# Moving the large tiles of a feed-forward pool by 384 bytes: from 416 to 288 modulo 512

## The chip, the core and the metric

The kernel runs on one core of a Trainium2 chip. The metric is the device time of one launch in microseconds (us), the median of several runs; less is better. All inputs are float32. The matrix products run on TensorE (PE) in the type float32r, from operands that VectorE (DVE) and ScalarE (ACT) have split into a high and a low part; SyncE (SP) and GpSimd (POOL) issue most of the DMAs.

## The reference, cut to what matters

One encoder block on 256 tokens of 2048 channels. Only its last half is touched by the change:

```
mix = merged @ w_out                                     # 2048 x 2048
h   = layernorm(ALPHA * x + mix, ln1_g, ln1_b)
ff  = square(relu(h @ w_ff1)) @ w_ff2                    # 2048 -> 8192 -> 2048
out = layernorm(ALPHA * h + ff, ln2_g, ln2_b)
```

Ahead of it stand the input projections (the stages `q`, `k`, `r`, `v`, `g`, `u` below), a gated linear attention, a Hyena convolution, and their output products.

## The kernel before

**How a product is made.** A weight is split into `hi` (a cast to float32r, on ACT) and `lo = weight - hi` (on DVE), the activation likewise; a product is the sum hi·hi + hi·lo + lo·hi. Two loops do this:

- `channel_products` (lines 141 to 153): the weight block is the stationary operand, the activation moves. Line 147 multiplies 128x128 of `whi` with 512 moving columns (256 tokens high and 256 tokens low), line 151 `wlo` with 256 columns. A block of 128 output channels is 16 matmuls of 512 columns and 16 of 256. The stages `q` and `k` and the first feed-forward product (`f<-hT,whi`) go this way.
- `token_products` (lines 188 to 201): the activation is stationary, 512 columns of the weight move. Lines 199, 200, 201 are the three terms. Most other stages go this way, and the last quarter of the second feed-forward product (`w<-whi,fa`).

**The feed-forward stage.** `ff1_first` makes 16 channel blocks of the first product (its first three begin in `begin_three`, lines 173 and 178). Then `ff_pairs` runs 48 slots, each with one channel block of the first product (32 matmuls) and seven "forms" of a seven-product scheme for the second (lines 1243 to 1245, three matmuls of 512 columns for each form: 21 matmuls). So a slot has 37 matmuls of 512 columns and 16 of 256. The stationary operand of the forms lies in `fa`: slots 0 to 3 of eight in `fa0`, 4 to 7 in `fa1` (eight products are summed before the next group starts). Their moving operand is, for three forms, `b_h` and `b_l` (tags `xh` and `wx`), for two `whi` and `wlo`, and for two the tails of `fa0` and `fa1`. After the slots the last quarter runs through `token_products` with `fa` as the stationary operand, half of it in `fa0`, half in `fa1`; its last group takes its weights from resident tiles (`xh_r`, `xl_r`, `fraw_r`, the tails of `fa`, and `wr`, which has the tag `hT`).

**What orders the work.** Inside a slot the instructions of ACT and DVE are pinned to the order of the program (`pin`, `VT`, `cast`). One bank of PSUM is left for the channel block of a slot, so its first matmul waits until `quad_sum` has read the block before (the row `DVE fr`). In eight slots of sixteen, `forms` adds work for the group to come, and in every eighth `take_sum` adds up the seven sums. The order of everything else is written by a planner that simulates the engines; the weights come by DMA some blocks ahead.

**Where tiles lie.** A pool lays its tags one behind the other in the order in which they are first asked for, each buffer rounded up to 32 bytes in a partition. The starts of the tiles in question, in bytes:

| tile (tag) | pool | start | modulo 512 |
|---|---|---|---|
| `dfth`, `dftl` | base | 5152, 7200 | 32 |
| `xT`, `mT`, `fa0` (`xT`) | base | 13600 | 288 |
| `yg`, `yh`, `zr` (`yT`) | base | 46368 | 288 |
| `raw`, `whi`, `wlo` | wp | 79392 and on | 32 |
| `bst` | ep | 128544 | 32 |
| `wx` (`b_l`) | ep | 128928 | 416 |
| `xh` (`b_h`, `xh_r`) | ep | 133024 | 416 |
| `xl` (even `fraw`, `xl_r`) | ep | 141216 | 416 |
| `f` (`wr1`, `fa1`) | ep | 149408 | 416 |
| `hT` (`wr3`) | ep | 182176 | 416 |
| `mv`, `lrs`, `rs_y`, `rs_t`, `rs_v`, `lnb` (two buffers each) | ep | 214944 to 215296 | - |
| `fr3`, `fr4`, `ft`, odd `fraw` | ep | 215328 and on | 288 |

All steps inside these tiles (a 512-column unit, a 128-column weight, a channel block, a slot of `fa`) are multiples of 512 bytes, so an operand starts at its tile's own value modulo 512. Of the other stages, these are used below: the filters' `hx` starts at 64 and `eoh`, `eol` at 32; the inverse transform's `Yh`, `Yl` at 32.

Of the kernel before, what the change touches and what calls it, by code (L numbers as in the profile page):

```python
# [9 lines left out]
F32 = mybir.dt.float32  # L10
# [6 lines left out]
P = 128  # L17
# [26 lines left out]
def block_kernel(  # L44
# [430 lines left out]
    for i in range(2 * NCH):  # L475
        c, o = divmod(i, 2)
        n = 4 + (i * 21) // 15
# [421 lines left out]
    ep = ctx.enter_context(tc.tile_pool(name="ep", bufs=1))  # L899
# [4 lines left out]
    def load_rows(i0):  # L904
        rows = zr[:, 2:4]
        for i in range(2):
            nc.scalar.dma_start(rows[:, i, :], ln_rows[i0 + i:i0 + i + 1, :].broadcast_to([P, D]))
        return rows
# [54 lines left out]
                            MM(ps, sl, hi[:, cs], start=False, stop=(kt == KT - 1))  # L963

    st1 = ep.tile([P, NT, 8, 6], F32, tag="bst", name="bst1")
    rows1 = load_rows(0)
    turn_b, turn_i = dfth, dftl
    for i, t in ((0, turn_b), (1, turn_i)):
# [435 lines left out]
    with tc.high_priority(), tc.issue_after(done.ins):  # L1404
        add_ff(pss[1][:, 0:256], 1, 1792, 256, last=True)
        mv = ep.tile([P, 2], F32, tag="mv", bufs=2, name="mvl")
# [160 lines left out]
```

## Time and profile before

| what | value |
|---|---|
| median of 3 runs | 1804.18 us (1803.63 to 1804.41) |
| profiled execution, its own time | 1803.89 us |
| its span, first to last instruction | 1802.1 us |
| TensorE busy | 1793.6 us |
| VectorE busy | 1455.6 us |
| ScalarE busy | 1039.2 us |
| granted TensorE clock | 0.999 |

The profile is one execution. A page of it gives the busy time of each engine, a chain of the work that ended last, and groups of instructions; the trace behind it can be asked for groups by line and shape, for waits, for a timeline and for stretches of time. A row of a group ends with count, busy time, mean duration in ns, and the idle time before it. Matmuls overlap, so the duration of one (some 390 ns for 512 columns) is longer than the distance from its start to the next one's; the distance is what adds up to the time, and it is read from the starts in the timeline. There, neighbours of one line are merged into one row with a count.

### The profile page before, as it was taken

Reading aid. Unit: us, or ns where it says so; the run is one execution under the profiler, and the core shown is the slowest. Engines: PE = TensorE matmul, PEld = TensorE weight load, DVE = VectorE, ACT = ScalarE, POOL = GpSimd, SP = SyncE. Lnnn points to the kernel's source line nnn. Section 1 sums busy time; section 2 is a strip of 40 time slices with the busy share of each in tenths; the row PEclk is TensorE's granted clock in tenths of the full one; section 3 lists DMA queues with packets and bytes.
Section 4 is the critical chain, followed back from the end, with each engine's and each line's share of the span. In section 5 each row is a group of like instructions: output and inputs, shape, how many; then the busy total and the mean of one; then the engine's idle time right before and its main releaser. Section 6 shows DMA issues by size and latency. Waiting matters only on the chain.

```text
span 1802.1 us, 23458 instructions
## 1 busy us (share of the span) xinstructions
PE 1793.6 (100%) x8787; PEld 1506.8 (84%) x8787; DVE 1455.6 (81%) x1869; ACT 1039.2 (58%) x1399; POOL 164.6 (9%) x217
## 2 busy tenths in 40 slices
PE   9999999999999999999999999999999999999998
PEld 7888888888888888888888889888888888888887
DVE  6789887875679989998845568687899889999867
ACT  6678768875344444445544445666667666665632
POOL 1011110000111101010000000001111111111100
PEclk9999999999999999999999999999999999999999
DMA  8668775455797979798555764568888888888663
GB/s 325 231 248 293 253 234 196 149 179 197 224 311 247 276 261 285 232 309 257 202 187 187 283 236 155 203 192 258 243 252 255 249 243 261 247 240 276 212 222 119
DMA packets 79281, 424.76 MB, mean 236 GB/s; under 512 B 9816, under 2 KB 12392, under 8 KB 38464
## 3 DMA queue, kind: packets, MB, share of 16 engines
q1 hardware_dynamic: 47808, 336.61, 50.5%
q0 software_dynamic: 24304, 66.99, 18.1%
q10 hardware_dynamic: 7056, 19.67, 3.0%
q8 instruction: 69, 1.13, 0.3%
q14 instruction: 44, 0.36, 0.1%
HBM read 381.86 MB, written 16.25 MB: 221 GB/s over the span
## 4 chain that ended last, share of the span: by engine, by line
PE 97%; DVE 2%; issue 0%; ACT 0%; DVEq 0%; ACTq 0%
PE f L147 12%; PE f L151 6%; PE w L1244 4%; PE w L1243 4%; PE w L1245 4%; PE g L200 3%; PE g L199 3%; PE g L201 3%; PE ux L200 3%; PE ux L199 3%; PE ux L201 3%; PE r L199 2%; PE r L200 2%; PE r L201 2%; PE k L147 2%; PE v L200 2%
## 5 line engine op out<-in xcount | busy, mean ns | idle before, releaser
L86 ACT CAST whi<-raw 128x1024 fp32r<-128x1024 f32 x392 | 412.5, 1053 | 412.9 <-PE ux L201 85.1
L87 DVE TENSOR_TENSOR wlo<-raw,whi 128x1024 fp32r<-128x1024 f32 x392 | 478.4, 1223 | 206.9 <-ACT whi L86 204.6
L147 PE MATMUL f<-hT,whi 128*128 128x512 f32 x984 | 246.9, 395 | 0.4 <-DVE fr L1102 0.4
L147 PEld LDWEIGHTS f<-hT,whi 128*128 128x128 f32 x984 | 180.7, 188 | 38.8 <-DVE fr L1102 0.8
L151 PEld LDWEIGHTS f<-hT,wlo 128*128 128x128 f32 x984 | 125.4, 188 | 5.6
L1102 DVE TENSOR_TENSOR wlo<-fraw,whi 128x1024 fp32r<-128x1024 f32 x96 | 117.3, 1222 | 13.5 <-ACT whi L1105 11.2
L151 PE MATMUL f<-hT,wlo 128*128 128x256 f32 x984 | 127.0, 282 | 0.0
L1105 ACT CAST whi<-ring 128x1024 fp32r<-128x1024 f32 x48 | 50.6, 1054 | 101.0 <-DVE ring L1102 97.6
L1168 POOL DMA_DIRECT2D ring<-wblk x48 | 41.7, 868 | 706.9 <-DVE ring L1102 706.9
L1105 ACT CAST whi<-fraw 128x1024 fp32r<-128x1024 f32 x96 | 100.7, 1049 | 0.1
L200 PE MATMUL g<-wlo,xT 128*128 128x512 f32 x256 | 100.2, 391 | 0.0
L201 PE MATMUL ux<-whi,xT 128*128 128x512 f32 x256 | 99.9, 390 | 0.0
L201 PE MATMUL g<-whi,xT 128*128 128x512 f32 x256 | 99.9, 390 | 0.0
L200 PE MATMUL ux<-wlo,xT 128*128 128x512 f32 x256 | 99.7, 389 | 0.0
L199 PE MATMUL g<-whi,xT 128*128 128x512 f32 x256 | 93.8, 392 | 0.0
L1105 ACT CAST b_h<-ring 128x1024 fp32r<-128x1024 f32 x96 | 75.2, 832 | 25.9 <-PE w L1245 21.5
L199 PE MATMUL ux<-whi,xT 128*128 128x512 f32 x256 | 89.7, 389 | 0.0
L1102 DVE TENSOR_TENSOR b_l<-ring,b_h 128x1024 fp32r<-128x1024 f32 x48 | 58.7, 1223 | 16.0 <-ACT b_h L1105 15.9
L1102 DVE TENSOR_TENSOR ring<-ring 128x512 f32<-128x512 f32 x96 | 66.2, 689 | 1.5
L1102 DVE TENSOR_TENSOR wlo<-ring,whi 128x1024 fp32r<-128x1024 f32 x48 | 58.8, 1225 | 1.9 <-ACT whi L1105 0.3
L1102 DVE TENSOR_TENSOR fa<-ring,fa 128x1024 fp32r<-128x1024 f32 x48 | 58.5, 1220 | 0.0
L1169 POOL DMA_DIRECT2D ring<-ring x48 | 58.1, 1210 | 0.0
(537 smaller groups left out, 4305.9 us busy)
## 6 DMA issues: line engine op xcount, KB each, us to landing
raw<-wblk SPq DMA_DIRECT2D x204, 1024.0 KB, 5.0
fraw<-wblk SPq DMA_DIRECT2D x48, 1024.0 KB, 4.8
ring<-wblk SPq DMA_DIRECT2D x48, 1024.0 KB, 7.1
Td<-T POOLq DMA_DIRECT2D x32, 384.0 KB, 5.4
conv_sb<-conv_rows SPq DMA_DIRECT2D x12, 1024.0 KB, 11.5
Tl<-Td POOLq DMA_DIRECT2D x16, 768.0 KB, 9.5
ring<-wblk POOLq DMA_DIRECT2D x48, 256.0 KB, 4.4
ring<-ring POOLq DMA_DIRECT2D x48, 256.0 KB, 5.1
```

The source lines that it names most:

```text
L86: return (nc.scalar.copy(hi, src), nc.vector.tensor_tensor(lo, src, hi.bitcast(F32), op=ALU.subtract))
L87: nc.vector.tensor_tensor(lo, src, hi.bitcast(F32), op=ALU.subtract))
L147: MM(ps[:, :, ts], hi[:, js], act[:, kt, :, ts], start=(kt == 0 and opens), stop=(kt == KT - 1))
L151: MM(ps[:, 0, ts], lo[:, js], act[:, kt, 0, ts], start=False, stop=False)
L199: MM(pss[tb], sh, wh, start=(kt == 0), stop=False)
L200: MM(pss[tb], sh, wl, start=False, stop=False)
L201: MM(pss[tb], sl, wh, start=False, stop=(kt == KT - 1))
L1102: return pin(nc.vector.tensor_tensor(dst, a, b, op=op))
L1105: return pin(nc.scalar.copy(hi, src))
L1243: pin(MM(ps, sh, wh, start=(i == 0), stop=False))
L1244: MM(ps, sh, wl, start=False, stop=False)
L1245: pin(MM(ps, sl, wh, start=False, stop=(i == 7)))
```

## The change

Right behind `bst`, the first tag of the pool `ep`, six small tags are asked for that the layer norms use later. They get their place there instead of behind `hT`: twelve buffers of 32 bytes, 384 bytes in all. The tiles `wx`, `xh`, `xl`, `f` and `hT` start 384 bytes later than before, at 288 modulo 512 (129312, 133408, 141600, 149792, 182560). `bst` and everything from `fr3` on stay where they are, and the pool is as large as before. No instruction is added or removed; of each tag with two buffers the layer norms take the other buffer first.

```diff
     st1 = ep.tile([P, NT, 8, 6], F32, tag="bst", name="bst1")
+    for tag, n in (("mv", 2), ("rs_y", 1), ("rs_t", 1), ("rs_v", 1), ("lrs", 1), ("lnb", 1)):
+        ep.tile([P, n], F32, tag=tag, bufs=2, name=f"first_{tag}")
     rows1 = load_rows(0)
```

## The prediction

> **What bounds the kernel.** I read the page first: the busy times, the granted clock, the chain that ended last.
>
> ```profile
> span 1802.1 us, 23458 instructions
> ...
> PE 1793.6 (100%) x8787; PEld 1506.8 (84%) x8787; DVE 1455.6 (81%) x1869; ACT 1039.2 (58%) x1399; POOL 164.6 (9%) x217
> ...
> PEclk9999999999999999999999999999999999999999
> ...
> PE 97%; DVE 2%; issue 0%; ACT 0%; DVEq 0%; ACTq 0%
> ```
>
> TensorE is never idle to speak of, at full granted clock, and 97% of the chain is its own. So only the distance between matmuls can change the time. The change moves operands and nothing else, so the question is whether that distance depends on where an operand lies. For this I took the groups by line and shape, and compared 512-column matmuls whose operands start at different places modulo 512 (the table of tiles).
>
> ```profile
> L147 PE MATMUL f<-hT,whi 128*128 128x512 f32 x984 | 246.9, 395 | 0.4 <-DVE fr L1102 0.4
> L200 PE MATMUL ux<-wlo,xT 128*128 128x512 f32 x256 | 99.7, 389 | 0.0
> L1243 PE MATMUL w<-fa 128*128 128x512 f32 x48 | 19.1, 398 | 0.0
> L334 PE MATMUL X<-hx,eol 128*128 128x512 f32 x32 | 12.7, 396 | 0.0
> L333 PE MATMUL yp<-Yh,dfth 128*128 128x512 f32 x32 | 12.5, 389 | 0.0
> ```
>
> All are the same shape, 128x512, yet there are two prices. 389 ns: `wlo` with `xT` (32 and 288, 256 bytes apart) and `Yh` with `dfth` (32 and 32). 395 or 396 ns: `hT` with `whi` (416 and 32, 384 apart), `hx` with `eol` (64 and 32). Cheap are pairs that start 0 or 256 bytes apart modulo 512, dear the others. `w<-fa` at 398 is an exception, 288 and 288 in slots that use `fa0`; I come back to it.
>
> Stages differ in much else, so I looked for both cases in one stage, and for distances instead of durations. In the last quarter, lines 199 to 201 use the same `whi` and `wlo`; only the stationary operand changes, from `fa0` (288) to `fa1` (416). The timeline of TensorE, columns start, time, line, operands, count; each half is 8 k-tiles x 2 token blocks x 3 terms, 48 matmuls:
>
> ```profile
> 1725.53 0.62 PE L199 MATMUL w<-whi,fa 128*128 128x512 f32 x2
> ...
> 1736.42 0.64 PE L199 MATMUL w<-whi,fa 128*128 128x512 f32 x2
> ...
> 1747.58 0.62 PE L199 MATMUL w<-whi,fa 128*128 128x512 f32 x2
> ```
>
> 1736.42 - 1725.53 = 10.89 us, 226.9 ns apiece, with `fa0`; 1747.58 - 1736.42 = 11.16 us, 232.5 ns, with `fa1`. Same line, moving tiles and work beside it: 5.6 ns for the address. That is the core of my reading.
>
> Are operands at one and the same place cheap too? After the change most forms have 288 and 288. Near the end `wr` and `fa1` meet, both at 416:
>
> ```profile
> 1776.69 0.39 PE L199 MATMUL w<-wr,fa 128*128 128x512 f32 x1
> ...
> 1780.32 0.39 PE L200 MATMUL w<-wr,fa 128*128 128x512 f32 x1
> ```
>
> 16 steps in 3.63 us, 226.9 ns. So I take 0 and 256 apart as one class.
>
> **The change, part by part.** Every moved tile goes from 416 to 288, so every pair of the feed-forward stage falls into the cheap class: `hT` with `whi` 288 and 32, the forms 288 and 288 or 32 and 288. I price each kind of work by the nearest row that has its alignment already.
>
> *A channel block.* `k` has the moving operand at 288 and `whi` at 32, just what `f` will have. First `k`, then `f`:
>
> ```profile
> 63.22 2.08 PE L151 MATMUL k<-xT,wlo 128*128 128x256 f32 x16
> 65.13 3.82 PE L147 MATMUL k<-xT,whi 128*128 128x512 f32 x16
> 68.79 0.40 PE L151 MATMUL k<-xT,wlo 128*128 128x256 f32 x2
> ```
>
> ```profile
> 1141.43 3.90 PE L147 MATMUL f<-hT,whi 128*128 128x512 f32 x16
> 1145.16 2.06 PE L151 MATMUL f<-hT,wlo 128*128 128x256 f32 x16
> 1147.07 3.88 PE L147 MATMUL f<-hT,whi 128*128 128x512 f32 x16
> 1150.79 2.06 PE L151 MATMUL f<-hT,wlo 128*128 128x256 f32 x16
> ```
>
> `k`: 1.91 + 3.66 = 5.57 us; `f`: 3.73 + 1.91 and 3.72 + 1.91, mean 5.63. A block gains 0.06. It is less than 16 x 5.6 = 90 ns, since the 3.66 holds a settling-in: 16 x 226.9 would be 3.63. The 256-column runs cost the same here, 1.91 and 1.91. 16 blocks lie outside the 46 slots counted below (14 in the opening of the stage, one each in the first and the last slot): 0.9 us.
>
> *A slot.* Now 8 slots from the third on, by stretches, then one slot in the timeline:
>
> ```profile
> 1212.09:1295.89 83.80, 83.80 (x425) 70.84 (x424) 68.24 (x77) 54.25 (x69) 14.05 (x16) 1.00 0.85 254
> ```
>
> ```profile
> 1411.17 2.03 PE L147 MATMUL f<-hT,whi 128*128 128x512 f32 x8
> ...
> 1416.79 0.40 PE L1243 MATMUL w<-fa 128*128 128x512 f32 x1
> ...
> 1421.66 0.63 PE L147 MATMUL f<-hT,whi 128*128 128x512 f32 x2
> ```
>
> A slot is 83.80 / 8 = 10.475 us, of which the 21 matmuls of the forms take 1421.66 - 1416.79 = 4.87, 232 ns each. After: 5.57 + 21 x 0.2269 = 10.335. A gain of 0.14 for a slot, 6.4 us over 46 slots. Here 15 of the 21 are at 288 and 288, priced by the 416/416 row; bounded from the other side, they stay at 232.
>
> *What DVE takes back.* The busy time of the 8 slots shows DVE (third number) at 68.24 of 83.80. That slack is gone in heavy slots, those with `forms` and sums. Two stretches, cut at slot starts, of five and of three slots; the waits of DVE in the first; the one wait of PE there:
>
> ```profile
> 1505.46:1558.37 52.91, 52.49 (x267) 44.09 (x265) 50.41 (x70) 32.94 (x46) 8.77 (x10) 1.00 0.78 246
> 1547.29:1558.37 11.08, 10.66 (x55) 8.67 (x53) 10.51 (x16) 5.74 (x10) 1.75 (x2) 1.00 0.77 237
> 1610.85:1642.58 31.73, 31.69 (x160) 26.50 (x159) 30.90 (x41) 18.16 (x24) 5.28 (x6) 1.00 0.75 235
> ```
>
> ```profile
> DVE fa L1102 <- ACT fa L1105: 1.4, 4, 0.4
> ```
>
> ```profile
> 1558.37 0.50 PE L147 MATMUL f<-hT,whi 128*128 128x512 f32 x1 [0.42 <-DVE fr L1102]
> ```
>
> In the first stretch DVE is busy 50.41 of 52.91 us and waits 1.4 more inside its own round with ACT (the two halves of `forms`), which PE doesn't enter. PE, done with its forms, waits for DVE's sum `fr` of the block before. A faster PE only waits longer there: I give the five slots no gain, and the three of the second stretch (30.90 of 31.73) none. Left are 46 - 8 = 38 slots x 0.14 = 5.3 us. The bounds: all 46 gain (6.4), or only about 25 lighter ones do (3.5).
>
> *The rest.* Three halves of the last quarter move from 11.16 to 10.89: 0.8 us. The closing group, 16.72 us for 73 starts of 512 columns and one of 256:
>
> ```profile
> 1764.06:1780.78 16.72, 16.72 (x74) 13.64 (x73) 12.62 (x16) 6.79 (x8) 0.00 (x0) 1.00 0.24 98
> ```
>
> At 226.9 it would take 16.4 or a little more: 0.3. The forms of the first two slots and the six that trail the last, 36 at 5 ns: 0.2. Lone 256-column matmuls at the ends (lines 173, 961 to 963, some 390) I cost at -0.2, half a ns each, between nothing and 1 ns.
>
> *At nothing:* the writes of ACT and DVE into the moved tiles, and the loads into `xl`, which are the only steady DMAs that move (24 of 48 `fraw` loads, begun two slots ahead). The two buffers of each small tag swap their turns; the two norms are far apart. If one of these did cost something, a light slot covers it: DVE idles some 2 us there (83.80 - 68.24 over 8).
>
> Sum: 0.9 + 5.3 + 0.8 + 0.3 + 0.2 - 0.2 = 7.3 us. The profiled execution took 1803.89 us, 1.8 around its span; the median is 0.3 above it. 1804.2 - 7.3 = **1796.9 us**.
>
> The Trainium skill speaks against all this: SBUF — State Buffer, "Who interferes with whom", gives TensorE two read ports, one for the moving operand and an independent one for weight loads, and says "PE and ACT never wait on anyone"; no tile's start would then matter, and the time would stay at 1804. Where the two halves of the last quarter differ by 0.27 us, this trace disagrees.
>
> **The rivals.**
>
> *No effect* (5%). The start of a tile doesn't set the distance, or the tags don't land where the diff says. Then dear rows are dear because of their stage, and nothing moves: 1804.2. Against it stand the two halves above, one stage and one line. By the rule of the Trainium skill above, this is the case that would come out.
>
> *Equal places stay dear* (10%). The row `w<-fa` at 398 ns has 288 and 288 in the slots of `fa0`. I read it as the settling-in after a dear neighbour, since its neighbours in the slot are 416 and 288. If instead equal starts at 288 are dear, 15 of 21 matmuls of a slot gain nothing: 0.06 + 6 x 5 ns = 0.09 a slot, 3.4 us over 38, and 0.9 + 0.8 + 0.2 - 0.2 with it: 5.1, so 1799.1. For it speaks that row, against it the `wr` rows.
>
> *DVE is the bound in every heavy slot* (6%). Only 25 slots gain: 3.5 + 2.0 = 5.5, so 1798.7. For it speaks the 50.41 of 52.91; against it that PE's matmuls of `f` waited for `fr` 0.4 us in the whole trace (the first group row).
>
> *Slower* (4%). The planner writes another order, as the six tiles change whose buffer is free when, and `fr` comes late in every heavy slot, as it did in the slot from 1547.29 to 1558.37, which lasted 11.08 instead of 10.475: 0.6 lost. In all 21 heavier slots that is 12.7 against 7.3 + 1.1 gained elsewhere at most: 1808.5 or so. It outweighs the gain from about 14 such slots on. Against it: the order of a slot is pinned by hand.
>
> **How the numbers follow.** Forecast 75%, the rivals 10, 6, 5 and 4. A measurement of this kernel tells 0.2%, 3.6 us, from no change; the forecast and two rivals lie beyond it: faster 0.91, same 0.05, slower 0.04. The range: below, all 46 slots gain (8.4) and the waits of DVE shrink or the settling-in falls away, some 1.3 more: 1794.4. Above, the two smaller gains with 1.2 us for terms that fail: 1800.3.
>
> **What would show it.** Right: `f<-hT,whi` falls from 395 to about 390 to 391 ns, the row of `k`; all `w` rows to 389 or 390; the halves of the last quarter become equal, 10.9 us each; 8 light slots take 82.7 us instead of 83.80; the slots from 1505 to 1558 keep their 52.9 us, with a longer wait of PE for `fr`. The stages ahead of 1080 us don't change. Wrong: `f` still at 395 (no effect); `w<-fa` and `w<-b_h` at 395 or more while `f` has fallen (equal places); waits for `fr` in many slots (DVE); another order of instructions.

## The result, and the profile after

| | median, us | lowest to highest | runs |
|---|---|---|---|
| before | 1804.17 | 1803.63 to 1804.41 | 5 |
| after | 1796.44 | 1796.17 to 1797.29 | 5 |

The ratio is 0.9958, 95% interval [0.9944, 0.9972]: 7.7 us less, where 7.3 were forecast (1796.9). The two kernels have the same instructions in the same order on all five engines; only addresses differ. Line numbers of the code behind the edit are 2 higher after (1243 to 1245 become 1245 to 1247, 1102 becomes 1104).

The page of after, the rows that answer to those of before (span, busy times, granted clock, shares of the chain):

```profile
span 1795.1 us, 23458 instructions
...
PE 1784.6 (99%) x8787; PEld 1506.7 (84%) x8787; DVE 1453.9 (81%) x1869; ACT 1037.7 (58%) x1399; POOL 164.7 (9%) x217
...
PEclk9999999999999999999999999999999999999999
...
PE 93%; DVE 3%; ACT 1%; DMA 1%; issue 1%; SPq 0%; DVEq 0%; POOL 0%; ACTq 0%
```

PE's busy time fell from 1793.6 to 1784.6 us at the same granted clock and the same 8787 matmuls. The other engines' busy times moved by 1.7 us at most. So the time came out of the matmuls. The groups of after by line and shape (count, busy us, mean ns of one, idle time ahead of them) say out of which:

```profile
L147 PE MATMUL f<-hT,whi 128*128 128x512 f32 x984 | 242.8, 391 | 1.1 <-DVE fr L1104 1.1
L151 PE MATMUL f<-hT,wlo 128*128 128x256 f32 x984 | 127.7, 283 | 0.0
L1245 PE MATMUL w<-fa 128*128 128x512 f32 x48 | 18.7, 389 | 0.0
L334 PE MATMUL X<-hx,eol 128*128 128x512 f32 x32 | 12.7, 396 | 0.0
```

`f` fell from 395 to 391 ns, and the form `w<-fa` from 398 to 389. `X<-hx,eol`, which the change doesn't touch, is at 396 as before. `f<-hT,wlo` is no cheaper. The distances, as before, from TensorE's timeline: two channel blocks, then the halves of the last quarter with `fa0` (first) and `fa1` (second).

```profile
1136.32 3.82 PE L147 MATMUL f<-hT,whi 128*128 128x512 f32 x16
1139.98 2.08 PE L151 MATMUL f<-hT,wlo 128*128 128x256 f32 x16
1141.89 3.82 PE L147 MATMUL f<-hT,whi 128*128 128x512 f32 x16
```

```profile
1719.20 0.62 PE L199 MATMUL w<-whi,fa 128*128 128x512 f32 x2
...
1730.08 0.62 PE L199 MATMUL w<-whi,fa 128*128 128x512 f32 x2
...
1740.96 0.62 PE L199 MATMUL w<-whi,fa 128*128 128x512 f32 x2
```

A block is 3.66 + 1.91 = 5.57 us, just the block of `k`. The halves are 10.88 and 10.88: the 0.27 us between them are gone. Now the stretches, cut at slot starts (length, then busy times of PE, PEld, DVE, ACT, POOL): eight light slots; the five and the three slots that were forecast to give nothing; and within the five the last.

```profile
1211.76:1294.37 82.61, 82.61 (x425) 70.91 (x424) 68.23 (x77) 54.32 (x70) 14.05 (x16) 1.00 0.86 259
1500.91:1553.84 52.93, 51.81 (x267) 44.08 (x265) 50.40 (x70) 32.93 (x46) 8.77 (x10) 1.00 0.81 247
1542.24:1553.84 11.60, 10.48 (x55) 8.67 (x53) 11.04 (x16) 6.27 (x10) 1.75 (x2) 1.00 0.76 225
1605.61:1637.52 31.91, 31.27 (x160) 26.51 (x159) 31.01 (x41) 18.36 (x25) 5.28 (x6) 1.00 0.75 235
```

A light slot is 82.61 / 8 = 10.33 us, before 10.475. The five slots still take 52.93 (before 52.91) and the three 31.91 (31.73). DVE's busy time in them is what it was; PE's fell (52.49 to 51.81, 31.69 to 31.27), and the difference is now waiting. The timeline at the end of each stretch shows for what:

```profile
1553.84 2.11 PE L147 MATMUL f<-hT,whi 128*128 128x512 f32 x8 [1.11 <-DVE fr L1104]
```

```profile
1636.26 0.50 PE L1246 MATMUL w<-wlo,fa 128*128 128x512 f32 x1 [0.64 <-DVE wlo L1104]
```

The wait for `fr` grew from 0.42 to 1.11 us, and a wait for `wlo` of 0.64 us is new.

### The profile page after: what moved, and what is told of

It is laid out like the page before. It is cut to its first block, busy times and chain, and to the rows that moved or that the text cites. A ratio compares the mean times of both kernels' runs of the same rounds, so it can differ in the third digit from the quotient of the medians.

```text
span 1795.1 us, 23458 instructions
## 1 busy us (share of the span) xinstructions
PE 1784.6 (99%) x8787; PEld 1506.7 (84%) x8787; DVE 1453.9 (81%) x1869; ACT 1037.7 (58%) x1399; POOL 164.7 (9%) x217
## 4 chain that ended last, share of the span: by engine, by line
PE 93%; DVE 3%; ACT 1%; DMA 1%; issue 1%; SPq 0%; DVEq 0%; POOL 0%; ACTq 0%
PE f L147 11%; PE f L151 6%; PE w L1246 4%; PE w L1247 4%; PE w L1245 4%; PE g L200 3%; PE g L199 3%; PE g L201 3%; PE ux L199 3%; PE ux L201 3%; PE ux L200 3%; PE k L147 2%; PE v L201 2%; PE v L200 2%; PE v L199 2%; PE ho L200 2%
## 5 line engine op out<-in xcount | busy, mean ns | idle before, releaser
L147 PE MATMUL f<-hT,whi 128*128 128x512 f32 x984 | 242.8, 391 | 1.1 <-DVE fr L1104 1.1
```

The lines of the kernel that those rows point to most:

```text
L147: MM(ps[:, :, ts], hi[:, js], act[:, kt, :, ts], start=(kt == 0 and opens), stop=(kt == KT - 1))
```

## The experiments

The theory: the distance between two matmuls depends on the gap, modulo 256 bytes, between the start of the moving operand and that of the stationary one, and nothing else in the change matters. Its rivals: the small tags in their other buffers or the other neighbours of the tiles are the cause; a tile's own place, without regard to its partner; and, for what was given back, something other than DVE. Where a variant adds 128 bytes or needs the room, the four last one-column tiles of the kernel (`fin0` to `fin3`) share the tags of `rs_y`, `rs_t`, `rs_v` and `lrs`. "Gap" below is the start of the moving operand less that of the stationary one, modulo 256. Each group of runs had runs of before beside it, with medians from 1803.62 to 1804.52 us, and each ratio is to those.

**1. Back at 416, the small tags staying in front.**

```diff
+    ep.tile([P, 32], F32, tag="pad", name="pad")
     rows1 = load_rows(0)
```

> The change with a pad of 128 bytes behind the six small tags: the small tags stay in front, the large tiles start at 416 again (and the last norm's four scratch words reuse the small tags, to make room). If the gap between the starts of the two operands decides: as before, 1804 us, f at 395 ns. If it were the order of the small tags or their buffers: as the change, 1796.5 us.

Measured: 1804.35 us (1803.76 to 1805.3, 10 runs), ratio to before 1.0002 [0.9993, 1.0012]. Its groups:

```profile
L147 PE MATMUL f<-hT,whi 128*128 128x512 f32 x984 | 246.9, 395 | 0.4 <-DVE fr L1105 0.4
L1246 PE MATMUL w<-fa 128*128 128x512 f32 x48 | 19.1, 398 | 0.0
```

395 and 398 as in before. The order of the tags and the swapped buffers do nothing that shows; the start decides.

**2. The other cheap place, without the change.** Before, with a pad of 128 bytes ahead of the large tiles, so that they start at 32.

> The kernel before with only a pad of 128 bytes behind bst: small tags where they were, large tiles at 32 modulo 512. If a gap of 0 is as cheap as one of 256 (the class counts modulo 256): 1796.5 us, f at 391 ns, forms at 389 ns. If 288 itself is what counts, or the small tags: 1804 us. If only a gap of 256 were cheap for f with whi (now 32 and 32): about 1800 us.

Measured: 1796.69 us (1796.31 to 1796.83), ratio 0.9958 [0.9943, 0.9973]; `f<-hT,whi` at 391, the rows `w<-fa` at 389. The gain comes whole, with the small tags where they were, and a gap of 0 between `hT` and `whi` is as good as one of 256.

**3. The gap or the place?** After, with all tiles of all pools 128 bytes further on, so that every start changes and no gap does.

```diff
+    base.tile([P, 32], F32, tag="pad", name="pad")
     eps_sb = base.tile([P, 1], F32, tag="eps", name="eps_sb")
```

> The change with 128 bytes ahead of everything in the first pool: all tiles start 128 bytes later, at 160 or 416 modulo 512, and no gap between two operands changes. If the gap decides: as the change, 1796.5 us, forms at 389 ns. If each tile's own place decides (416 is dear by itself): nearly all 512-column matmuls of the kernel get dear, some 6000 at 5.6 ns, about 1830 us.

Measured: 1796.41 us (1795.83 to 1797.26), ratio 0.9957 [0.9942, 0.9972]; `f` 391 and `w<-fa` 389 again. `fa1` now lies at 416, the place that was dear before, and is cheap. So it is the gap between the two operands, for shifts of 128 bytes at least.

**4. Only `hT`.** Before, with the six tags asked for just ahead of `hT`: `hT` goes to 288, while `wx`, `xh`, `xl` and `fa1` stay at 416.

> The six small tags asked for just before hT: only hT moves to 288, the tiles xh, xl, wx and fa1 stay at 416. If each matmul is priced by its own pair: a channel block gains 0.06 us, 62 blocks 3.5 us less what VectorE takes back in eight slots: about 1801 us, blocks of the opening at 5.57 us. If the settling-in after dear neighbours spreads into the block: half of it in the slots, about 1802.3 us.

Measured: 1802.31 us (1801.08 to 1804.01, 10 runs), ratio 0.999 [0.998, 0.9999]. In the opening, where blocks follow one another, a block takes the whole gain (5.567 us). In the slots it depends on the forms ahead of it. The timeline of two slots, at the starts of their blocks, of their forms and of the next slot:

```profile
1399.89 1.98 PE L147 MATMUL f<-hT,whi 128*128 128x512 f32 x8
...
1405.46 0.39 PE L1245 MATMUL w<-fa 128*128 128x512 f32 x1
...
1410.31 2.01 PE L147 MATMUL f<-hT,whi 128*128 128x512 f32 x8
...
1415.91 0.39 PE L1245 MATMUL w<-fa 128*128 128x512 f32 x1
...
1420.76 2.01 PE L147 MATMUL f<-hT,whi 128*128 128x512 f32 x8
```

The first block takes 5.57 us, the second 5.60, of 5.62 in before. Ahead of the first stand forms of `whi` and `wlo` with `fa0`, at gap 0; ahead of the second the same forms with `fa1`, at gap 128, and two thirds of the block's gain are gone. Half of the slots are of each kind. So the gap of one matmul is paid in part by the matmuls behind it. That is also how `w<-fa` came to 398 ns at a gap of 0: its tile hasn't moved in this variant, only the block ahead of it has become cheap, and the row falls to 389.

```profile
L1245 PE MATMUL w<-fa 128*128 128x512 f32 x48 | 18.7, 389 | 0.0
```

**5. Half-way.** After with a pad of 64 bytes: the large tiles at 352, gap 64.

> The change with a pad of 64 bytes: large tiles at 352, 64 bytes off the cheap class. If only gaps of 0 and 256 are cheap: dear again, f at 395 to 396 ns, about 1804 us. If the price grows with the distance from the cheap class up to 128: half of it, f at 393 ns, about 1800 us. If a gap of 64 still is cheap: 1796.5 us.

Measured: 1800.45 us (1799.82 to 1802.85, 10 runs), ratio 0.9981 [0.9971, 0.999]. The groups:

```profile
L147 PE MATMUL f<-hT,whi 128*128 128x512 f32 x984 | 244.7, 393 | 0.5 <-DVE fr L1105 0.5
L151 PE MATMUL f<-hT,wlo 128*128 128x256 f32 x984 | 125.5, 279 | 0.0
L1248 PE MATMUL w<-fa 128*128 128x512 f32 x48 | 19.0, 396 | 0.0
```

The total is about half-way, but it isn't made of halves: the 21 forms of a slot are as dear as in before (by their starts 4.86 us on the mean, before 4.85, after 4.76), `f` of 512 columns is between, and the 256-column products are cheaper than in either kernel, 279 ns against 282 and 283.

**6 and 7. Two more starts**, to see whether the price follows the distance from a multiple of 256: after with 32 bytes (start 320), and before with 64 (start 480).

> The kernel after with a pad of 32 bytes, so that the large tiles of the feed-forward pool begin at 320 modulo 512, 32 bytes from the cheap gap to whi and wlo (the stage X with hx against eol had the same gap of 32 before, at 396 ns). Theory A, only gaps that are multiples of 256 are cheap and any other is dear: f near 395, about 1803 to 1804. Theory B, the price grows with the distance from such a multiple: 64 bytes gave half of the gain back (1800.45), so 32 gives a quarter: about 1798.4, f near 392.

> The kernel before with a pad of 64 bytes, so that the large tiles begin at 480 modulo 512, 64 bytes from the cheap gap on the other side than at 352. Theory A, price by the distance from the nearest multiple of 256, the same on both sides: as at 352, 1800.45, with cheaper 256-column matmuls (279 ns). Theory B, it matters which operand lies ahead: as dear as at 416 or dearer, 1804 or more, 256-column matmuls at 282 or more.

Measured: 320 gave 1803.37 us (1802.44 to 1804.12, 10 runs), ratio 0.9994 [0.9985, 1.0003], and 480 gave 1798.31 (1798.1 to 1800.09, 5 runs), ratio 0.9968 [0.9956, 0.998]. First the groups of 320, then those of 480:

```profile
L147 PE MATMUL f<-hT,whi 128*128 128x512 f32 x984 | 247.3, 395 | 0.4 <-DVE fr L1105 0.4
L151 PE MATMUL f<-hT,wlo 128*128 128x256 f32 x984 | 125.3, 279 | 0.0
```

```profile
L147 PE MATMUL f<-hT,whi 128*128 128x512 f32 x984 | 247.0, 395 | 0.7 <-DVE fr L1103 0.7
L151 PE MATMUL f<-hT,wlo 128*128 128x256 f32 x984 | 122.3, 277 | 0.0
```

For 512 columns both are as dear as 416: a gap of 32 costs what 128 costs, and the price doesn't grow with the distance. Theory B falls at 320. At 480 neither theory holds: the 256-column products come closer together than anywhere, and make most of the gain: the busy time of `f<-hT,wlo` falls from 127.0 to 122.3 us. A run of 16 of them takes 1.82 us there, in the timeline of 480:

```profile
1144.04 1.98 PE L151 MATMUL f<-hT,wlo 128*128 128x256 f32 x16
1145.85 3.89 PE L147 MATMUL f<-hT,whi 128*128 128x512 f32 x16
1149.58 1.98 PE L151 MATMUL f<-hT,wlo 128*128 128x256 f32 x16
1151.40 3.89 PE L147 MATMUL f<-hT,whi 128*128 128x512 f32 x16
```

1151.40 - 1149.58 = 1.82 us, 114 ns apiece, half of the cheap 227 of 512 columns; in after it is 1.91, 120 apiece. The 512-column run beside it takes 1149.58 - 1145.85 = 3.73, the dear price. At this start the two shapes don't want the same gap.

**8. What DVE takes back.** After, with the `forms` of four of each eight blocks one slot later:

```diff
-    FORMED = {... enumerate((10, 11, 13, 14, 16, 17, 19, 20))}
+    FORMED = {... enumerate((10, 11, 13, 14, 17, 18, 20, 21))}
```

> The change with four of the eight formings of a group one slot later (17, 18, 20, 21 instead of 16, 17, 19, 20), so that none falls into the slot with the last two sums. If VectorE's load in that slot is what TensorE waits for at the long slot: it falls from 11.60 to 10.4 or so, 1795.2 us. If the wait has another cause (the ring's loads): no change, 1796.5 us. If the later formings run into the next sums: slower, 1797 or more.

Measured: 1795.04 us (1794.19 to 1795.71), ratio 0.995 [0.9938, 0.9963]; after's runs all lie above these, though the before of this group, at 1803.87 us, is 0.3 us faster than that of after's. In the profiled executions the 46 slots take 475.81 us, 1.6 less than in after. The five slots that took 52.93:

```profile
1501.32:1552.98 51.66, 51.66 (x267) 44.26 (x265) 48.87 (x66) 32.52 (x44) 8.79 (x10) 1.00 0.83 253
```

51.66 us, the five at 10.33 to 10.35 each; PE is busy throughout. DVE has 48.87 us to do in them instead of 50.40, and no wait for `fr` is left among the waits of PE.

**9. The same cure in other stages.** After, with pads that bring the filters' and the attention's own tiles (`hx`, `wb`, `l`, `sth` and `stl` among them) to 288 or 32 modulo 512.

```diff
+        fp.tile([P, 56], F32, tag="pad", name="padf")
...
+    gp.tile([P, 40], F32, tag="pad", name="padg")
...
+                    gp.tile([P, 56], F32, tag=f"pad{d}", name=f"padg{d}")
```

> The change with pads in the pools of the filters and of the attention, so that hx, wb, l1, l2, ws, sth and stl start at 288 or 32 as well. If the gap decides there too: the rows X fall from 394 to 397 ns to about 390, o from 394 to 396 to 389, and their neighbours in r, v, k stop settling in: 1 to 3 us, about 1794.5 us. If these stages wait for their side work instead: no change, 1796.5 us.

Measured: 1794.62 us (1794.23 to 1795.52), ratio 0.9948 [0.9936, 0.9961]; again after's runs all lie above (the before is that of 8). `X` has come down from 396 to the cheap price, in stages that have nothing to do with the feed-forward:

```profile
L334 PE MATMUL X<-hx,eol 128*128 128x512 f32 x32 | 12.5, 389 | 0.0
```

Summed over the distances in the two traces, `r` gives 0.6 us, `X` 0.4, `o` and `v` 0.3 each, `k` and `g` 0.1 each: some 1.8 us, as much as the medians differ by.

**10. Both at once.** The edits of 8 and 9 together.

> The kernel after with both sides of its remaining loss taken at once: the later forms (which gave 1.4 us alone) and the filters' tiles at 288 (which gave 1.8 alone). Theory: one works on DVE's load in two slots, the other on the distance of TensorE's matmuls in other stages, so the gains add: 1796.4 - 1.4 - 1.8 = 1793.2 us. Rival: the measured 1.4 is partly scatter of one build, since a slot that waits 1.28 can give back no more than that and the sums of the following slots move too: 1793.8 to 1794.6, no better than the filters' tiles alone.

Measured: 1793.34 us (1792.55 to 1796.62, 5 runs), ratio 0.9944 [0.9931, 0.9958]. The median is the sum of the two gains (1793.2 expected). It is the fastest kernel of the study by its median, 3.1 us under after; one of its five runs is as slow as after's, and the intervals overlap, so the sum is likely and not settled.

**11. Each product at its own best gap.** From 480 it looked as if `wlo` should lie 64 bytes further on than `whi`: gap 0 for the products of `whi`, 192 for the 256-column products of `wlo`. The edits of 8 and 9 are kept (the second pad of 9 is 64 bytes shorter, as its pool now starts 64 further on), the large tiles start at 32, and:

```diff
+        hi = wp.tile([P, D // 2], F32R, tag="whi", bufs=3, name=f"whi{n}_{h}")
+        if not padded:
+            padded.append(wp.tile([P, 16], F32, tag="pad", bufs=1, name="padw"))
+        return hi, wp.tile([P, D // 2], F32R, tag="wlo", bufs=3, name=f"wlo{n}_{h}")
```

> A step from what the start at 480 showed: there the 256-column products with wlo (gap 192) came 114 ns apart instead of 120, while the 512-column ones with whi (gap 192 too) were dear at 233. Here every wlo tile lies 64 bytes further on, and the large tiles begin at 32: whi keeps the gap 0 throughout, wlo has 192 as the weight of k, q and f, and 64 where it is the moving operand of the other products (some 1440 matmuls); later forms and filters' tiles as in the kernel with both. Theory: each product is priced by its own gap alone. 256-column products gain 16 x 6.3 ns a block, 74 blocks: -7.4 us; 1440 moving ones lose the 3 ns that the start at 352 showed for gap 64: +4.3; some 200 lone ones +0.6. 1793.3 - 2.5 = 1790.8 us, f<-hT,wlo at 277. Rival: the price hangs on the change from one gap to the next, so that a row of whi and wlo in turn pays a settling-in at each step: the 1440 and their neighbours lose 5 ns and more each, some 8 to 20 us, 1794 to 1806.

Measured: 1813.47 us (1812.75 to 1813.93), ratio 1.0053 [1.0039, 1.0067]: 20 us slower than 10, and slower than before. The theory fell; the time lies beyond even the rival's range, but what the rival named, neighbours that pay where the gap changes, is what the rows show. Groups of a stage in which `whi` and `wlo` take turns as the moving operand, first one of before, then two of this variant:

```profile
L201 PE MATMUL g<-whi,xT 128*128 128x512 f32 x256 | 99.9, 390 | 0.0
```

```profile
L204 PE MATMUL g<-wlo,xT 128*128 128x512 f32 x256 | 101.2, 395 | 0.0
L205 PE MATMUL g<-whi,xT 128*128 128x512 f32 x256 | 101.0, 394 | 0.0
```

Only `wlo` has a gap of 64 here; `whi` lies at 32 against 288 as ever, yet it costs 394 ns where before it cost 390. The timeline of that stage, one matmul of line 203 and a later one with eight others between them:

```profile
420.06 0.40 PE L203 MATMUL g<-whi,xT 128*128 128x512 f32 x1
...
422.15 0.40 PE L203 MATMUL g<-whi,xT 128*128 128x512 f32 x1
```

2.09 us for nine steps, 232 ns each: all three terms pay the full price of a wrong gap, although two of the three have the right one. Over the 4,080 matmuls of lines 203 to 205 some 5 ns each are 20 us, which is about the loss. And the 256-column products at gap 192 came to 118 ns, not to the 114 of start 480 (281 ns a piece in the groups, where 277 was expected): the gap modulo 256 alone doesn't fix their price.

## Why the prediction was right

| stretch | forecast, us | measured, us |
|---|---|---|
| 14 blocks from the opening's fourth on, with the 30 forms among the last two | 14 x 0.06 + 30 x 5 ns = 0.99 | 0.67 (first twelve) + 0.29 = 0.95 |
| 46 slots | 5.3 | 5.48 (482.88 to 477.39) |
| from the last slot's block to the end | 0.06 + 0.8 + 0.3 + 0.03 - 0.05 = 1.1 | 1.17 (107.15 to 105.99) |
| all that stands ahead | -0.15 | -0.63 (1124.56 to 1125.19) |

The table compares the two profiled executions, which differ by 7.0 us; the medians differ by 7.7, and the forecast was 7.3. The -0.2 for lone 256-column matmuls is split by where they stand, some three quarters of them ahead of the fourth block.

**What bounds.** The premise, that only the distance between matmuls counts, held: PE's busy time fell by 9.0 us, of which 7.0 arrived in the span of the profiled execution. The rest went into waits, among them the 0.7 and 0.6 us at the ends of the two stretches above and 0.6 in an earlier stage.

**The price of an address.** 226.9 against 232.5 ns was read off two halves of one stage. After, both halves are at 10.88 / 48 = 226.7 ns, and experiments 1, 2 and 3 exclude the tags, the buffers and a tile's own place (for shifts by 128 bytes). The dear class of the prediction, every gap that isn't 0 or 256, held for 512 columns at 32, 128 and 192. At 64 it failed in part: there `f` comes out between (experiment 5).

**A block and a slot.** `k` as the model of `f` was exact, 5.57 us; the slot came to 10.33 for 10.335. The 0.06 of a block, less than 16 x 5.6 ns, was put down to a settling-in, and the starts show one (the last section). Experiment 4 shows that cost from the other side, where a cheap block behind dear forms keeps 0.02 of its gain instead of 0.06. It explains a slot, too: in before some half of its 21 forms had a gap of 0 already (with `fa0` those of `whi`, `wlo` and the tail of `fa0`; with `fa1` those of `b_h`, `b_l` and the tail of `fa1`), and yet all 21 stood 231 ns apart on the mean. So the prediction was right to price all of them by what the row took, and not by the count of wrong pairs. Two small misreadings did no harm: the 256-column runs don't cost the same, 1.90 us in before and 1.91 after, and the closing group has 72 starts of 512 columns and not 73; it went from 16.72 to 16.46 us.

**Equal places** (10%) are cheap: all forms at 288 and 288 stand at 389. The row at 398, which spoke for this rival, was a matmul of gap 0 that paid for the dear block ahead of it, as the prediction had read it; experiment 4 shows it at 389 once that block is cheap.

**What DVE takes back.** The two stretches were named with their lengths, and both kept them to 0.2 us, with longer waits of PE. For the five slots that wait was caused by DVE's load: to do four of each eight `forms` one slot later removed it (experiment 8). The form of the loss is worth a look: four of the five slots gained some 0.12 us each, and the fifth paid all of it back (11.08 to 11.60). For the three slots the new wait, for `wlo`, was not tried by itself: it is 0.4 us in the profile of experiment 8 and missing in that of 10, and its cause is open. The rival in which DVE binds in every heavy slot (6%) had the mechanism and the wrong count: two slots of 21 wait.

**No effect** (5%) is dead with the result. The Trainium skill's SBUF — State Buffer, "Who interferes with whom", by which TensorE's two read ports are independent, would have left after at 1804 as the prediction read it, with no start that matters. After at 1796.4 and experiment 1 at 1804.4 differ by the starts of the large tiles, a spare pad and the shared tags of four one-column tiles; experiments 2 and 3 have such a pad and the same shared tags and stand at 1796.7 and 1796.4. So here the measurement decides against that reading.

**Slower** (4%): the planner wrote the same order, and `fr` came late in one slot, as it had before.

**What failed.** "The stages ahead of 1080 us don't change": up to the opening's fourth block the profiled execution took 0.6 us longer, with one wait that before doesn't have, of `hb` (line 422) for ACT's `T`, 0.6 us. Of the variants only that of experiment 8 shows it. Nothing in that stage was edited, and its cause is open. It may be scatter: in the profiles of the variants that leave these stages as they are, the first matmul of `f` starts anywhere from 1105.1 us (start 480) to 1106.9 (experiment 8), in before at 1106.0 and in after at 1106.5. The term of 0.2 for lone 256-column matmuls had the right direction: in lines 173, 178 and 961 to 963 the distances grew by 0.6 to 1.1 ns, 0.3 us in all.

**What stays open** is the mechanism. That the weight load of the next matmul and the moving stream of this one meet in something with a period of 256 bytes would fit experiments 1 to 3; it is argued, not shown. Nor do the runs tell apart whether the weights in use or those of the next matmul count, since in a row of one stage both come from the same tile. Such a meeting doesn't explain by itself why a single dear product in three makes all three dear (11), nor the prices of 256 columns.

## What to carry to other kernels

When TensorE is busy for nearly the whole span, look at the distance between starts of equal matmuls in one stage: a few ns between two halves that differ only in a tile is a price of the tile's address, here 2.4% of the distance (5.6 of 232.5 ns) and 0.4% of the kernel. For float32r products like these, lay the moving and the stationary tiles of every product of a stage at one gap (0 modulo 256 bytes was right here for 512 columns), and not only those of most: one wrong product in three cost the whole row. Then look where the gain is given back: heavy slots of another engine return it at their end, and a later start of a little of that engine's work kept it.

## What the runs showed of the hardware that was not expected

- The distance in a run of 16 products of 256 columns depends on the start of the moving tile in another way than that of 512 columns: 120 ns at gap 0, 119 at 128 (before), 117 at 32 and 64, 114 at start 480. At 512 columns the means over a run of 16 are 228, 233, 233, 229 and 233 ns (gaps 0, 128, 32, 64, and start 480).
- In a stage whose moving operand changes between gaps 0 and 64, the distances of all three products are 233 ns on the mean (`g` in experiment 11; 229 in before), those at gap 0 too.
- A change between shapes or gaps costs a few matmuls until the steady distance is reached: behind a run of 256 columns the first five distances of 512 columns are 233, 236, 228, 233 and 231 ns in after, the rest 227. In experiment 4 a block of gap 0 behind forms of gap 128 shows the like over all of its first eight (234, 236, 224, 231, 236, 228, 232 and 231 ns); behind forms of gap 0 they stand at 227.
